# Issuing a weight sum behind the remainder of the unit ahead of it, in a four-layer trunk

## The chip, the cores and the metric

The kernel runs on one core of one Trainium2 chip. The metric is device microseconds (us) of that core, the median over the runs shown. TensorE is PE in the profile (PEld is its weight load), VectorE is DVE, ScalarE is ACT, GpSimd is POOL, and SyncE is SP.

## The reference

A residual stream of 256 tokens by 2048 channels passes a latent attention layer, an MLP, a state-space (Mamba-2) layer and a second MLP. All of it is float32. What the change touches are products of activations with large weights.

```python
def squared_relu_mlp(h, w_in, w_out):
    u = jax.nn.relu(h @ w_in)          # 2048 x 8192
    return (u * u) @ w_out             # 8192 x 2048

def ssm_mixer(h, w_in, ...):
    zxbcdt = h @ w_in                  # 2048 x 10304
    ...
    return y @ w_out

for i in range(DEPTH):                 # DEPTH = 2
    ...
    x = x + mix
    h = rms_norm(x, mlp_norm_g[i])
    x = x + squared_relu_mlp(h, mlp_w_in[i], mlp_w_out[i])
```

## The kernel before

**Weight units.** Weights stream in from HBM as units of 128x1024 float32 (512 KB, two blocks of 128x512). TensorE takes float32 operands in a reduced form (fp32r), so each unit is split: ScalarE writes an upper part `wh` (line 102), VectorE subtracts it from the raw weight and writes the remainder `wl` (line 103). A product then needs three matmuls, upper by upper, upper by remainder, and activation remainder by weight upper (lines 617 to 619 in the MLP, 1160 to 1162 in the state-space layer). A unit's matmuls follow a list that is fixed ahead of time. When TensorE's code takes unit j, the code for the split of unit j+3 is issued (`Flow.next`, with `ahead` giving how many units are loaded and split ahead). `wh` and `wl` have four buffers each, raw weights have six, so the split of a unit can only start when TensorE is done with the unit four places before it.

**Units with sums.** Eight column pairs of the first matrix of each MLP, seven of them woven with other work, and two pairs of the state-space input matrix are computed by a scheme of seven products in place of eight (`seven`). For one pair there are four slices d = 0 to 3, and for each slice four quarters of weights b11, b12, b21, b22. The units that the list takes in each slice, one after the other with other units between them, are

- M1: b11 as it was loaded, in a buffer of the pool `rx`;
- N7: b12 + b22, written over b22, both fresh from HBM, in two buffers of the pool `raw`;
- N5: b11 + b12, written over b12;
- N6: b11 + the new b22, written over b11. A GpSimd DMA (line 199) then accumulates b21 onto that buffer for the later unit N4;
- N4, M2 and N3 follow later, and need no VectorE sum.

Each sum is one VectorE instruction of 128x1024 (all have line 183, that of the helper `add`). The pairs of the MLPs are p = 1 to 7 in each of the two MLPs, those of the state-space layer are p = 0 and 1. That makes 56 + 8 = 64 rounds of M1, N7, N5, N6, so 64 sums for N7. In the profile a sum for N7 is the group `wraw<-wraw,wraw`, one for N5 `wraw<-wrx,wraw`, one for N6 `wrx<-wrx,wraw`.

**What sets the order.** TensorE's order is written out by hand (`manual_schedule`). On VectorE, ScalarE and the DMA queue of SyncE a scheduler of the framework places an instruction by its own estimate of when it can start. Once placed, each engine works through its queue in order, and an instruction that waits holds up all behind it. A call of `issue_after(ins)` adds an edge without a semaphore: what is issued inside it stands behind `ins` in the queue of that engine. `flow.last_lo` is the latest remainder (line 103) that was issued, which at the split of N7 is that of the unit before it in the list.

**Other work on the same queues.** Between the splits VectorE adds finished output blocks to the residual (`add_residual`, line 437), subtracts for the transposed hidden activations (line 300) and combines bank results (lines 621, 622). ScalarE has relu and square (577, 625, 567), the upper parts of the transposed activations (299), and a copy of the bank of M1 to SBUF at the end of a pair's M1 products (line 631, in `after`).

Of the kernel before, what the change touches and what calls it, by code (L numbers as in the profile page):

```python
# [71 lines left out]
class Flow:  # L72
# [22 lines left out]
    def halves(self, raw, n, step=None):  # L95

        nc = self.nc
        h = self.pools["wh"].tile([P, 1024], F32R, tag="wh", name=f"wh{self.done}")
        lo = self.pools["wl"].tile([P, 1024], F32R, tag="wl", name=f"wl{self.done}")
        for o in range(0, n, step or n):  # L100
            v = slice(o, o + (step or n))
            self.last = nc.scalar.activation(h[:, v], raw[:, v], AF.Copy)  # L102
            self.last_lo = nc.vector.tensor_tensor(lo[:, v], raw[:, v], h[:, v].bitcast(F32), ALU.subtract)  # L103
        return h, lo
# [65 lines left out]
def seven(prefix, p, src):  # L170

    state = {}

    def quarter(d, i, j):
        return src[2 * i + d // 2, 2 * p + j][:, (d % 2) * 1024:(d % 2) * 1024 + 1024]

    def unit(flow, name, d):  # L180
        nc = flow.nc
        st = state.setdefault(d, {})
        add = lambda out, a, b: nc.vector.tensor_tensor(st[out].tile, st[a].tile, st[b].tile, ALU.add)
        halves = lambda q: flow.halves(st[q].tile, 1024)

        def make():
            if name == "N7":
                add("b22", "b12", "b22")
                out = halves("b22")
                if d in LATE5:  # L190
                    nc.gpsimd.dma_start(st["b12"].tile, quarter(d, 0, 0), accum_op=ALU.add)
                return out
            if name == "N5" and d not in LATE5:
                add("b12", "b11", "b12")
                return halves("b12")
            if name == "N6":
                add("b11", "b11", "b22")
                out = halves("b11")
                nc.gpsimd.dma_start(st["b11"].tile, quarter(d, 1, 0), accum_op=ALU.add)  # L199
                return out  # L200
            return halves({"M1": "b11", "N4": "b11", "N5": "b12"}.get(name, name))

        def load(k, pool, q):
            st[k] = Load(pool, quarter(d, *q))
            return st[k]

        loads = {"M1": lambda: [load("b11", "rx", (0, 0))],
                 "N7": lambda: [load("b12", B12, (0, 1)), load("b22", "raw", (1, 1))],
                 "M2": lambda: [load("M2", "raw", (1, 0))], "N3": lambda: [load("N3", "raw", (1, 1))]}
        return Unit(prefix + (p, name, d), 2, 512, loads.get(name, list)(), make)  # L210

    return unit


class Trunk:
# [224 lines left out]
    def start(self, seq):  # L440
        nc, d = self.nc, self.d
        self.flow = Flow(nc, self.wp, seq, (6, 3))
        cst = self.c.tile([P, C_END], F32, name="cst")
        self.cst = cst
        self.ident_r = self.c.tile([P, P], F32R, name="ident")
        self.ident = self.ident_r.bitcast(F32)
        self.mhalf = self.c.tile([P, 16], F32, name="mhalf")
        warm = self.s2.tile([P, 512], F32R, tag="s2", name="warm")
        nc.vector.memset(warm.bitcast(F32), 1.0)
        bank = self.sm.tile([P, 512], F32, tag="sm", name="warmed")  # L450
        for _ in range(WARM):
            nc.tensor.matmul(bank, warm[:, :P], warm, start=True, stop=True)
        nc.gpsimd.memset(self.mhalf, -0.5)
        nc.scalar.dma_start(cst[:, C_G0:C_GQ], d["cst"][:, C_G0:C_GQ])
        nc.scalar.activation(self.stat(1), self.mhalf[:, :1], AF.Copy)
        raws = [self.ktile(self.k4, F32) for _ in range(4)]
        parts = [(0, slice(k, k + 1)) for k in range(4)] + [(1, slice(0, 2)), (1, slice(2, 4)), (2, slice(0, 4)), (3, slice(0, 4))]

        def some_x():
            j, k = parts.pop(0)  # L460
            nc.sync.dma_start(raws[j][:, k], d["xT"][j][:, k])

        self.flow.load(2, ((0, 512), (512, 1024)), some_x)
        for u in range(3, 7):
            some_x()
            self.flow.load(u)
        self.pos = self.c.tile([P, 2], I32, name="pos")
        self.x = [[self.res.tile([P, 512], F32, name=f"x{t}{n}") for n in range(4)] for t in range(2)]

        self.rs_pool = [self.c.tile([P, 4], F32, name=f"rs{i}") for i in range(2)]  # L470
        self.phase = 0
        self.xT = [(self.ktile(self.xtp), self.ktile(self.xtp)) for _ in range(4)]

        def split_x(j, ks):
            h, lo = self.xT[j]
            for k in ks:
                g = cst[:, C_G0 + 4 * j + k:C_G0 + 4 * j + k + 1]
                if (j, k) == (0, 0):
                    nc.vector.tensor_scalar(h[:, k], raws[j][:, k], g, None, ALU.mult)
                else:  # L480
                    nc.scalar.activation(h[:, k], raws[j][:, k], AF.Copy, scale=g)
                nc.vector.scalar_tensor_tensor(lo[:, k], raws[j][:, k], g, h[:, k].bitcast(F32), ALU.mult, ALU.subtract)

        split_x(0, (0,))
        self.flow.convert(1)
        split_x(0, (1, 2))
        self.flow.convert(2)
        split_x(0, (3,))
        self.flow.load(7)
        one = self.scratch()  # L490
        nc.sync.dma_start(one[:, :P], d["one"])
        nc.gpsimd.tensor_copy(self.ident_r, one[:, :P])
        nc.sync.dma_start(cst[:, C_GQ:], d["cst"][:, C_GQ:])
        nc.sync.dma_start(self.pos, d["pos"])
        split_x(1, range(4))
        ssq = self.stat(8)
        self.later(0, lambda: split_x(2, range(4)))
        self.later(1, lambda: split_x(3, range(4)))

        def stats(n):  # L500
            for t in range(2):
                nc.sync.dma_start(self.x[t][n], d["x"][t * P:(t + 1) * P, n * 512:(n + 1) * 512])
                self.square_sum(self.x[t][n], ssq[:, t * 4 + n:t * 4 + n + 1])
            if n == 3:
                self.set_rstd(ssq)

        for n, at in enumerate(X_AT):
            self.later(at, lambda n=n: stats(n))
# [1299 lines left out]
```

## Time and profile before

| | us |
|---|---|
| median of 3 runs | 2289.38 (2289.05 to 2290.42) |
| the profiled execution | 2292.69 |
| its span, first to last instruction | 2290.9 |
| mean granted TensorE clock | 0.999 |
| ACT busy | 1442.6 (63%) |
| POOL busy | 284.9 (12%) |
| HBM read | 542.23 MB |

A page of the profile gives busy time by engine, the chain of work that ended last, and groups of instructions by source line. In a group's row the numbers are count, busy us, mean ns of one, and the idle time of its engine just before it with what ended that. In the view of waits a row reads: engine, operation, what it waited for, us in total, times, longest. In the timeline a row reads: start, us, engine, line, operation, tiles, and in brackets the idle time before it. A "q" after an engine's name marks its instruction queue.

A matmul of 512 columns is shown with 0.39 us, but the next one starts 0.23 us later, since they overlap. So idle time of PE as shown is 0.16 us less than what was lost at that place.

### The profile page before, as it was taken

The page shows a single profiled execution, that of the slowest core. Times are in us where ns is not written, and L with a number is a line of the kernel's source. Part 1 is how long each engine was busy: PE and PEld are TensorE (multiplying, and loading weights), DVE is VectorE, ACT ScalarE, POOL GpSimd, SP SyncE. Part 2 cuts the span into 40 slices and gives each one's busy share as a digit, 9 for nine tenths or more (in the row PEclk, how much of TensorE's full clock was granted, in tenths as well). Part 3 has the DMA queues.
Part 4 walks back from the last instruction along what each step waited for, and adds up shares of the span by engine and source line. Part 5 has one row for each costly group of instructions (what it writes and reads, how often), then busy time and mean ns, then how long its engine had stood idle before and what let it go on. Part 6 is the DMA issues. An engine that isn't in the chain of part 4 may idle for free.

```text
span 2290.9 us, 30854 instructions
## 1 busy us (share of the span) xinstructions
PE 2273.1 (99%) x10881; PEld 1881.4 (82%) x10881; DVE 1964.4 (86%) x2257; ACT 1442.6 (63%) x2044; POOL 284.9 (12%) x339
## 2 busy tenths in 40 slices
PE   9999999999999999999999999999999999999999
PEld 7898888888888888887788788888888887888887
DVE  7786698999899897888889998976989988989985
ACT  7775476566566666566577676564666665666663
POOL 1440000000000000100002532230000000000000
PEclk9999999999999999999999999999999999999999
DMA  8545678888888877758798888866788887798874
GB/s 315 172 152 163 210 234 264 261 253 263 269 253 261 268 231 246 244 180 281 234 359 288 290 289 303 307 215 218 211 261 252 256 275 234 253 277 243 266 232 163
DMA packets 176026, 569.74 MB, mean 249 GB/s; under 512 B 20192, under 2 KB 29344, under 8 KB 175872
## 3 DMA queue, kind: packets, MB, share of 16 engines
q1 hardware_dynamic: 147808, 498.24, 64.9%
q0 software_dynamic: 16320, 56.88, 11.8%
q10 hardware_dynamic: 11744, 12.66, 1.7%
q8 instruction: 85, 1.39, 0.2%
q14 instruction: 69, 0.57, 0.1%
HBM read 542.23 MB, written 6.41 MB: 239 GB/s over the span
## 4 chain that ended last, share of the span: by engine, by line
PE 87%; DVE 6%; DMA 4%; issue 2%; ACT 1%; POOL 0%; SPq 0%; ACTq 0%; DVEq 0%
PE acc L339 10%; PE acc L340 10%; PE acc L343 10%; PE yp L618 9%; PE yp L619 8%; PE yp L617 8%; PE st L618 7%; PE st L619 7%; PE st L617 7%; DVE wl L103 3%; DMA wraw<-mi 2%; DMA wraw<-si 1%; ACT wh L102 1%; PE st L1162 1%; PE st L1160 1%
## 5 line engine op out<-in xcount | busy, mean ns | idle before, releaser
L102 ACT ACTIVATE wh<-wraw 128x1024 fp32r<-128x1024 f32 (+1 forms) x818 | 857.5, 1053 | 528.5 <-PE acc L340 176.7
L103 DVE TENSOR_TENSOR wl<-wraw,wh 128x1024 fp32r<-128x1024 f32 (+1 forms) x818 | 989.2, 1227 | 180.5 <-ACT wh L102 169.7
L617 PE MATMUL yp<-wh,k 128*128 128x512 f32 x896 | 349.7, 390 | 0.0
L618 PE MATMUL yp<-wl,k 128*128 128x512 f32 x896 | 349.1, 390 | 0.1
L619 PE MATMUL yp<-wh,k 128*128 128x512 f32 x896 | 349.0, 390 | 0.0
L102 ACT ACTIVATE wh<-wrx 128x1024 fp32r<-128x1024 f32 x192 | 203.2, 1059 | 174.8 <-PE yp L619 98.4
L103 DVE TENSOR_TENSOR wl<-wrx,wh 128x1024 fp32r<-128x1024 f32 x192 | 233.0, 1219 | 37.1 <-ACT wh L102 36.2
L618 PEld LDWEIGHTS yp<-wl,k 128*128 128x128 f32 x896 | 168.5, 188 | 35.5 <-DVE wl L103 0.5
L619 PEld LDWEIGHTS yp<-wh,k 128*128 128x128 f32 x896 | 168.5, 188 | 35.2
L339 PE MATMUL acc<-wh,k 128*128 128x512 f32 x496 | 196.9, 397 | 0.3 <-ACT k L299 0.3
L617 PEld LDWEIGHTS yp<-wh,k 128*128 128x128 f32 x896 | 168.5, 188 | 34.9
L340 PE MATMUL acc<-wh,k 128*128 128x512 f32 x496 | 193.7, 391 | 0.6 <-DVE k L300 0.6
L339 PE MATMUL acc<-wh,xt 128*128 128x512 f32 x480 | 191.8, 400 | 0.6 <-ACT wh L102 0.6
L340 PE MATMUL acc<-wh,xt 128*128 128x512 f32 x480 | 187.7, 391 | 0.0
L617 PE MATMUL st<-wh,xt 128*128 128x512 f32 x448 | 177.7, 397 | 0.0
L619 PE MATMUL st<-wh,xt 128*128 128x512 f32 x448 | 174.9, 390 | 0.0
L618 PE MATMUL st<-wl,xt 128*128 128x512 f32 x448 | 174.7, 390 | 0.0
L199 POOL DMA_DIRECT2D wrx<-mi x56 | 49.1, 877 | 726.1 <-DVE wl L103 515.5
L617 PE MATMUL st<-wh,sN 128*128 128x512 f32 x336 | 133.4, 397 | 0.8 <-ACT wh L102 0.8
L618 PE MATMUL st<-wl,sN 128*128 128x512 f32 x336 | 131.8, 392 | 2.1 <-DVE wl L103 2.0
L343 PE MATMUL acc<-wl,k 128*128 128x512 f32 x496 | 132.7, 389 | 0.0
L619 PE MATMUL st<-wh,sN 128*128 128x512 f32 x336 | 131.4, 391 | 0.0
(342 smaller groups left out, 3806.6 us busy)
## 6 DMA issues: line engine op xcount, KB each, us to landing
wraw<-mi SPq DMA_DIRECT2D x256, 512.0 KB, 5.7
wraw<-mo SPq DMA_DIRECT2D x256, 512.0 KB, 5.2
wraw<-si SPq DMA_DIRECT2D x160, 512.0 KB, 5.7
wraw<-so SPq DMA_DIRECT2D x64, 512.0 KB, 5.1
wrx<-mi SPq DMA_DIRECT2D x56, 512.0 KB, 5.2
wrx<-mi POOLq DMA_DIRECT2D x56, 512.0 KB, 7.7
wraw<-wo SPq DMA_DIRECT2D x32, 512.0 KB, 4.1
tap<-xD SPq DMA_DIRECT2D x24, 512.0 KB, 8.3
```

The source lines that it names most:

```text
L102: self.last = nc.scalar.activation(h[:, v], raw[:, v], AF.Copy)
L103: self.last_lo = nc.vector.tensor_tensor(lo[:, v], raw[:, v], h[:, v].bitcast(F32), ALU.subtract)
L199: nc.gpsimd.dma_start(st["b11"].tile, quarter(d, 1, 0), accum_op=ALU.add)
L339: nc.tensor.matmul(accs[t][:, :n], ah, wh[:, q, :], start=first and kt + q == 0, stop=False)
L340: nc.tensor.matmul(accs[t][:, :n], al, wh[:, q, :], start=False, stop=False)
L343: nc.tensor.matmul(accs[t][:, :n], lhs(kt + q, t)[0], wl[:, q, :], start=False, stop=en and q == nk - 1)
L617: nc.tensor.matmul(b, ah, wh, start=first and q == 0, stop=False)
L618: nc.tensor.matmul(b, ah, wl, start=False, stop=False)
L619: nc.tensor.matmul(b, al, wh, start=False, stop=last and q == 1)
L1160: nc.tensor.matmul(bank[onto], ah, wh, start=done + q == 0 and not skip, stop=False, skip_group_check=skip)
L1162: nc.tensor.matmul(bank[onto], ah, wl, start=False, stop=done == 3 and q == 1, skip_group_check=skip)
```

## The change

Two places change. The sum for N7 is issued inside `issue_after` with the last remainder, so it stands behind that remainder in VectorE's queue. The context is handed to the flow object.

```diff
         def make():
             if name == "N7":
-                add("b22", "b12", "b22")
+                with flow.tc.issue_after(flow.last_lo.ins):
+                    add("b22", "b12", "b22")
                 out = halves("b22")
...
         self.flow = Flow(nc, self.wp, seq, (6, 3))
+        self.flow.tc = self.tc
```

No instruction is added or removed. TensorE's and GpSimd's orders are the same, on SyncE one load moves (a b11 quarter of the state-space layer, behind four other loads). What moves on VectorE and ScalarE is shown at three places. Names carry buffer numbers that are the same in both kernels; line numbers above 188 are one or two higher in the changed kernel.

On VectorE, second half of pair 0 of the state-space layer (about 1049 to 1060 us in the trace of before). `wraw_9766` is the sum for N7 of slice d = 3, `wl_9729` the remainder of N5 and `wl_9742` that of N6 of slice d = 2, `wl_9789` that of M1 of slice 3. Before:

```order
L103 TENSOR_TENSOR wl_9711<-wraw_9669,wh_9710 128x1024
L183 TENSOR_TENSOR wrx_9655<-wrx_9655,wraw_9669 128x1024
L183 TENSOR_TENSOR wraw_9766<-wraw_9764,wraw_9766 128x1024
L103 TENSOR_TENSOR wl_9729<-wraw_9667,wh_9728 128x1024
L183 TENSOR_TENSOR wraw_9764<-wrx_9752,wraw_9764 128x1024
L103 TENSOR_TENSOR wl_9742<-wrx_9655,wh_9741 128x1024
L103 TENSOR_TENSOR wl_9755<-wraw_9707,wh_9754 128x1024
L103 TENSOR_TENSOR wl_9769<-wrx_9554,wh_9768 128x1024
L103 TENSOR_TENSOR wl_9779<-wraw_9738,wh_9778 128x1024
L103 TENSOR_TENSOR wl_9789<-wrx_9752,wh_9788 128x1024
```

The same place with the change:

```order
L103 TENSOR_TENSOR wl_9711<-wraw_9669,wh_9710 128x1024
L183 TENSOR_TENSOR wrx_9655<-wrx_9655,wraw_9669 128x1024
L103 TENSOR_TENSOR wl_9729<-wraw_9667,wh_9728 128x1024
L103 TENSOR_TENSOR wl_9742<-wrx_9655,wh_9741 128x1024
L103 TENSOR_TENSOR wl_9755<-wraw_9707,wh_9754 128x1024
L103 TENSOR_TENSOR wl_9769<-wrx_9554,wh_9768 128x1024
L103 TENSOR_TENSOR wl_9779<-wraw_9738,wh_9778 128x1024
L103 TENSOR_TENSOR wl_9789<-wrx_9752,wh_9788 128x1024
L183 TENSOR_TENSOR wraw_9766<-wraw_9764,wraw_9766 128x1024
L183 TENSOR_TENSOR wraw_9764<-wrx_9752,wraw_9764 128x1024
```

The sum for N7 moves behind six remainders, to its place behind M1's, and the sum for N5 moves with it.

On VectorE, pair 2 of the first MLP, slice d = 2 and what follows (about 504 to 513 us). `wl_5026`, `wl_5051` and `wl_5064` are the remainders of N7, N5 and N6, `wrx_4955` is the sum for N6, `x_142` and `x_146` are residual adds of a finished output block. Before:

```order
L183 TENSOR_TENSOR wrx_4955<-wrx_4955,wraw_4975 128x1024
L103 TENSOR_TENSOR wl_5026<-wraw_4975,wh_5025 128x1024
L103 TENSOR_TENSOR wl_5038<-wraw_4993,wh_5037 128x1024
L103 TENSOR_TENSOR wl_5051<-wraw_4973,wh_5050 128x1024
L103 TENSOR_TENSOR wl_5064<-wrx_4955,wh_5063 128x1024
L103 TENSOR_TENSOR wl_5075<-wraw_5035,wh_5074 128x1024
L437 TENSOR_TENSOR x_142<-yp_4953,x_142 128x512
L437 TENSOR_TENSOR x_146<-yp_4954,x_146 128x512
L183 TENSOR_TENSOR wraw_5106<-wraw_5104,wraw_5106 128x1024
```

With the change:

```order
L183 TENSOR_TENSOR wraw_4975<-wraw_4973,wraw_4975 128x1024
L183 TENSOR_TENSOR wraw_4973<-wrx_4955,wraw_4973 128x1024
L103 TENSOR_TENSOR wl_5026<-wraw_4975,wh_5025 128x1024
L103 TENSOR_TENSOR wl_5038<-wraw_4993,wh_5037 128x1024
L103 TENSOR_TENSOR wl_5051<-wraw_4973,wh_5050 128x1024
L183 TENSOR_TENSOR wrx_4955<-wrx_4955,wraw_4975 128x1024
L438 TENSOR_TENSOR x_142<-yp_4953,x_142 128x512
L438 TENSOR_TENSOR x_146<-yp_4954,x_146 128x512
L103 TENSOR_TENSOR wl_5064<-wrx_4955,wh_5063 128x1024
L103 TENSOR_TENSOR wl_5075<-wraw_5035,wh_5074 128x1024
```

All three sums stand later, and the two residual adds now stand ahead of the remainder of N6. This sequence (sum for N6, two residual adds, remainder of N6) stands in the changed order eight times, four times in each MLP, and never in the order of before.

On ScalarE, slice d = 3 of pair 1 of the first MLP (about 333 to 340 us). `wh_3578`, `wh_3598` and `wh_3611` are the upper parts of M1, N7 and N5, `s_451` is the copy of the bank of M1, which reads what TensorE finishes with M1's last matmul. Before:

```order
L102 ACTIVATE wh_3578<-wrx_3520 128x1024
L299 ACTIVATE k_445_3557<-sm_3588 128x4x128
L102 ACTIVATE wh_3598<-wraw_3535 128x1024
L102 ACTIVATE wh_3611<-wraw_3533 128x1024
L102 ACTIVATE wh_3623<-wrx_3343 128x1024
L631 ACTIVATE s_451_3633<-st_3319 128x512
L299 ACTIVATE k_445_3557<-sm_3635 128x4x128
```

With the change:

```order
L102 ACTIVATE wh_3578<-wrx_3520 128x1024
L300 ACTIVATE k_445_3557<-sm_3588 128x4x128
L633 ACTIVATE s_451_3633<-st_3319 128x512
L102 ACTIVATE wh_3598<-wraw_3535 128x1024
L300 ACTIVATE k_445_3557<-sm_3635 128x4x128
L102 ACTIVATE wh_3611<-wraw_3533 128x1024
L102 ACTIVATE wh_3623<-wrx_3343 128x1024
```

The copy of M1's bank moves ahead of three upper parts, and one upper part of activations ahead of two of them. Pair 1 of the second MLP has the same move.

## The prediction

> **What bounds the kernel.** I read the page first, then the waits of VectorE and of TensorE, then timelines at the places that they name.
>
> ```profile
> span 2290.9 us, 30854 instructions
> PE 2273.1 (99%) x10881; PEld 1881.4 (82%) x10881; DVE 1964.4 (86%) x2257; ACT 1442.6 (63%) x2044; POOL 284.9 (12%) x339
> ```
>
> TensorE is busy for all but 17.8 us of the span, so the kernel is bound by its matmuls, and a change of order can win only what TensorE loses in waits. VectorE comes second with 86%, and its queue is in order.
>
> ```profile
> DVE wraw L183 <- DMA wraw<-mi: 23.3, 25, 2.7
> DVE wraw L183 <- DMA wraw<-si: 11.7, 7, 3.1
> PE st L1162 <- DVE wl L103: 4.5, 5, 1.4
> PE st L618 <- DVE wl L103: 2.0, 4, 0.8
> PE st L617 <- ACT wh L102: 0.8, 1, 0.8
> PEld st L1162 <- DVE wl L103: 7.0, 6, 1.8
> PEld st L618 <- DVE wl L103: 4.9, 9, 1.1
> PEld st L617 <- ACT wh L102: 1.7, 2, 1.3
> ```
>
> Half of the 64 sums for N7 (25 + 7 rows) stand at the head of VectorE's queue before their weights have landed, and hold it for 35.0 us in total. TensorE feels little of that: 4.5 + 2.0 + 0.8 = 7.3 us of shown idle time at ten places where it wants a remainder or an upper part of a pair's unit. One of them in full, VectorE first:
>
> ```profile
> 1053.32 1.23 DVE L183 TENSOR_TENSOR wraw<-wraw,wraw 128x1024 f32<-128x1024 f32 x1 [2.30 <-DMA wraw<-si]
> 1054.46 1.22 DVE L103 TENSOR_TENSOR wl<-wraw,wh 128x1024 fp32r<-128x1024 f32 x1
> 1055.73 0.50 PE L1162 MATMUL st<-wl,sN 128*128 128x512 f32 x1 [1.40 <-DVE wl L103]
> ...
> 1061.27 1.22 DVE L103 TENSOR_TENSOR wl<-wrx,wh 128x1024 fp32r<-128x1024 f32 x1
> ```
>
> VectorE was free from 1051.02, stood 2.30 us in front of the sum, then summed, and only then made the remainder of N5 that TensorE was waiting for. The remainder ended at 1055.68 and the matmul began 0.05 us later; I use that handover below.
>
> **What the change removes.** At that place the order shows the sum behind six remainders, behind that of M1, which is the last row, some 8 us later; the longest wait of a sum was 3.1 us. So its data are there, and the remainder of N5 can start at 1051, over 3 us earlier than it did, which is more than the 1.56 us that TensorE lost (1.40 shown plus the 0.16 by which matmuls overlap). The other places are of the same kind. I count all ten as gone: 7.3 + 10 x 0.16 = 8.9 us. PEld's rows bound it from above: 17 weight loads waited 7.0 + 4.9 + 1.7 = 13.6 us, but a load that waits has usually a matmul still running beside it; the seven without an idle row of PE lost under 0.16 us each, 1.1 us in all. I take 10.0; the ends are 7.3 and 13.6.
>
> **What the half-rate stretch adds.** Right behind one of the ten stands a stretch at half clock.
>
> ```profile
> 1054.00:1058.00 4.00, 1.99 (x8) 1.05 (x6) 4.00 (x5) 1.86 (x2) 0.00 (x0) 1.00 0.47 125
> 1904.50:1908.50 4.00, 2.38 (x8) 1.43 (x9) 3.95 (x4) 2.80 (x4) 0.18 (x1) 1.00 0.71 218
> 1908.60:1911.90 3.30, 3.30 (x9) 2.51 (x8) 3.30 (x4) 2.54 (x3) 0.62 (x1) 0.50 0.72 119
> ```
>
> By column: stretch, its length, busy time of PE, PEld, DVE, ACT and POOL with counts, granted clock, DMA share, GB/s. After 4.0 us with PE busy for 2.38 it ran 3.30 us at clock 0.50, which loses half of it, 1.7 us. The same density at 1054 (1.99 of 4.0) had no such sequel, so it takes more than the density, and I cannot say what. The Trainium skill ("TensorE: Matmul & The Clock Gate", part 1 and its table of rules) has the clock fall after about an idle window of 3.4 us and warns of idle gaps above some 3 us. This trace fell to half after two shown gaps below 1 us each, so here the row decides; by the page no new half-rate stretch could follow from the gaps that I work out below, and the sum would be 0.85 us lower. I count the stretch as gone and as likely as not to come back once at one of the two new places: minus 0.85 us, ends minus 1.7 and plus 1.7.
>
> **What the change adds, first kind.** A sum that used to run early, while VectorE waited for ScalarE or the DMA, now runs after M1's remainder, and everything of that round after it. At eight places two residual adds now stand between the sum for N6 and its remainder.
>
> ```profile
> 508.36 1.22 DVE L103 TENSOR_TENSOR wl<-wrx,wh 128x1024 fp32r<-128x1024 f32 x1 [0.18 <-ACT wh L102]
> 510.81 1.28 DVE L437 TENSOR_TENSOR x<-yp,x 128x512 f32<-128x512 f32 x2
> 510.87 0.39 PE L619 MATMUL yp<-wh,k 128*128 128x512 f32 x1
> 512.68 0.39 PE L618 MATMUL st<-wl,sN 128*128 128x512 f32 x1
> ```
>
> Before, the remainder of N6 was done at 509.58, and TensorE read it at 512.68: over 3 us of margin. Now the second residual add has to wait for the last matmul of its bank, which ends at 510.87 + 0.39 = 511.26. VectorE takes the next instruction 0.60 us after that add's start (two take 1.28, so one takes 0.68 and they overlap by 0.08), at 511.87; the remainder needs 1.22, and with the handover TensorE can read it at 513.14: 0.46 us late. The order of TensorE is the same at all eight places, so 8 x 0.46 = 3.7 us. Below nothing it cannot go; if the scheduler's place for the adds costs their full 1.28 us each time, it is 10 us.
>
> **Second kind.** In slice 3 of pair 1 the copy of M1's bank has moved ahead of the upper parts of N7 and N5.
>
> ```profile
> 334.40 2.00 ACT L102 ACTIVATE wh<-wraw 128x1024 fp32r<-128x1024 f32 x2
> 337.65 0.60 ACT L631 ACTIVATE s<-st 128x512 f32<-128x512 f32 x1 [0.30 <-PE st L619]
> 338.15 0.59 ACT L299 ACTIVATE k<-sm 128x512 fp32r<-128x512 f32 x1
> 337.81 0.48 PE L617 MATMUL st<-wh,sN 128*128 128x512 f32 x1
> 338.13 0.40 PE L618 MATMUL st<-wl,sN 128*128 128x512 f32 x1
> 339.51 0.39 PE L618 MATMUL st<-wl,sN 128*128 128x512 f32 x1
> 1673.62 0.60 ACT L631 ACTIVATE s<-st 128x512 f32<-128x512 f32 x1 [0.32 <-PE st L619]
> 1673.78 0.48 PE L617 MATMUL st<-wh,sN 128*128 128x512 f32 x1
> ```
>
> The copy waits for TensorE's last matmul of M1 and cannot start before 337.65. Behind it ScalarE is free at 338.15. The upper part of N7, which used to run from 334.40, now runs from 338.15 for 1.05 (two take 2.00, one starts 0.95 after the other), to 339.20, and TensorE starts N7 at 339.24 in place of 337.81: 1.43 late. The remainder then runs 339.24 to 340.46 and is read at 340.51 in place of 338.13: 2.38 late. For N5, ScalarE first does the 0.59 of line 299 (from 339.10), then the upper part to about 340.6; VectorE has the matching subtraction of line 300 first, so the remainder of N5 starts near 341.0, ends at 342.2, and TensorE, which would want it at 339.51 + 2.38 = 341.89, loses 0.36 more. That is 2.74 us in the first MLP. In the second, copy and N7 stand the same 0.16 us apart, so 2.74 again. The sums just before add a few tenths in the first. I take 5.8 us for both; if the copy cost only its own place it would be 2 x 1.43 = 2.9, and at twice the working 11.
>
> **What hides the rest.** In the other MLP rounds the sum lies in VectorE time that is free, as the margin shows.
>
> ```profile
> 487.63 1.21 DVE L103 TENSOR_TENSOR wl<-wrx,wh 128x1024 fp32r<-128x1024 f32 x1
> 488.77 2.35 DVE L103 TENSOR_TENSOR wl<-wraw,wh 128x1024 fp32r<-128x1024 f32 x2
> 492.27 0.39 PE L618 MATMUL st<-wl,sN 128*128 128x512 f32 x1
> ```
>
> Here M1's remainder is followed by N7's, done at 488.77 + 1.21 = 489.98 and read at 492.27, 2.29 us later. With the change the sum (1.14 from start to start), the upper part (1.05) and the remainder (1.22) follow M1's remainder in series, 3.4 us and two handovers behind its end at 488.84: 492.35. That would be 0.1 us late if M1's remainder stayed where it is. But the sums for N7 and N5, which stood ahead of it, have moved behind it, so M1's remainder can come up to 2 x 1.14 = 2.3 us earlier, and I expect a margin above 1 us. I cost the 46 rounds of this kind at nothing, and so the eight rounds of the state-space pairs, where six remainders stand ahead of the sum and the margin is wider. The cover is that margin; if it is gone, the second rival below has the price.
>
> ```profile
> wraw<-mi SPq DMA_DIRECT2D x256, 512.0 KB, 5.7
> ```
>
> Raw buffers are now read later by their sums, and so come free later, and one load is issued behind four others. A load lands 5.7 us after its issue (median), and the sums waited for theirs only because they stood so early; I cost both at nothing.
>
> **The sum.** Minus 10.0 minus 0.85 plus 3.7 plus 5.8 is minus 1.4 us on the profiled execution's own 2292.69, so 2291.3. Carried to the median of the runs, 2289.38, which is 3.3 lower, it gives 2288.0.
>
> **Rivals.** First: only the gain appears, because VectorE and ScalarE, no longer held for 35.0 us, reach the ten added places early enough. For it speaks the size of the 35.0; against it, both added waits hang on TensorE's own last matmul, which no earlier VectorE changes. Price: minus 10.0 and minus 1.7, so 2277.7. Chance 0.15, a part of it with some of the added waits left.
>
> Second, on the other side: the series sum, upper part, remainder uses up the margin in all rounds. It decides once M1's remainder does not come earlier by at least the 0.1 us above. With 0.3 us lost in each of the 46 rounds it adds 13.8 us: 2301.8. For it speaks that VectorE shows 86% over the whole span; against it, the removed 35.0 us. Chance 0.09.
>
> Third: the change does not do what it says, the queue still stands for the DMA at the new place, and only the added 9.5 us show: 2298.9. Against it, a sum waited at most 3.1 us and moved by more than that. Chance 0.04.
>
> **Chances.** My forecast has 0.72, with its own range 2284 to 2292. A measurement of this kernel can tell about 0.2%, or 4.6 us, from no change. Faster than 2284.8 takes the first rival and 0.05 of the forecast: 0.20. Slower than 2294.0 takes the other two rivals less their mildest part: 0.12. The rest is 0.68. The range runs from 2280.5, which takes in the milder half of the first rival, to 2293.5.
>
> **What would show it.** The rows of the sum for N7 waiting for a DMA should be gone from VectorE's waits, and PE's idle rows at lines 1162 and 618 near 1055, 1102, 1117, 1908 and 1994 with them. New idle rows should stand at eight reads of N6 remainders (near 513), 0.3 us each as shown, and at N7 in slice 3 of pair 1 near 339 and 1675, over 1 us each for upper part and remainder. I am wrong if the ten old waits stay, if rounds other than those ten show PE waiting for line 103, or if more half-rate stretches appear than one.

## The result, and the profile after

The changed kernel takes 2292.86 us (median of 22 runs, 2289.72 to 2297.09) beside 2289.22 us for the kernel before (22 runs, 2287.05 to 2294.09). The ratio is 1.0014 with a 95% interval of 1.0007 to 1.002, so the change costs 3.2 us (1.6 to 4.6). (The ratio is taken over all the runs of both, so it is not quite that of the two medians, which lie 3.6 us apart; all differences below go by such ratios.) The forecast was a gain of 1.4 us; the time lies inside the range, on the other side of no change.

The profiles of the two kernels say something else at first sight. The span of the changed kernel's is 2290.2 us, 0.7 us shorter than that of the one before.

```profile
span 2290.2 us, 30868 instructions
PE 2273.2 (99%) x10881; PEld 1881.4 (82%) x10881; DVE 1968.2 (86%) x2257; ACT 1434.2 (63%) x2044; POOL 284.5 (12%) x339
```

In the view of waits, the rows of a sum for N7 waiting for a DMA are gone from VectorE's, and TensorE's rows of the state-space pairs with them. What is left of TensorE's waits in the pairs is this:

```profile
PE st L620 <- DVE wl L103: 4.6, 12, 0.8
PE st L619 <- ACT wh L102: 2.4, 2, 1.2
```

That is 7.0 us shown, fourteen waits at ten places, where before it was 7.3 us in ten waits: old waits went, new ones came. In the state-space pair that the prediction shows, VectorE (timeline, start and length in us) now makes four remainders in a row and finds the sum's data there:

```profile
1048.80 2.35 DVE L103 TENSOR_TENSOR wl<-wraw,wh 128x1024 fp32r<-128x1024 f32 x2
1051.07 2.35 DVE L103 TENSOR_TENSOR wl<-wrx,wh 128x1024 fp32r<-128x1024 f32 x2
1053.34 1.22 DVE L183 TENSOR_TENSOR wraw<-wraw,wraw 128x1024 f32<-128x1024 f32 x1
```

The first of the two sorts of new waits, pair 2 of the first MLP (TensorE is some 4.6 us later here than in the trace of before):

```profile
515.22 1.37 DVE L438 TENSOR_TENSOR x<-yp,x 128x512 f32<-128x512 f32 x2 [0.25 <-PE yp L621]
516.50 1.22 DVE L103 TENSOR_TENSOR wl<-wrx,wh 128x1024 fp32r<-128x1024 f32 x1
517.06 0.39 PE L619 MATMUL st<-wh,sN 128*128 128x512 f32 x1
517.78 0.50 PE L620 MATMUL st<-wl,sN 128*128 128x512 f32 x1 [0.33 <-DVE wl L103]
518.11 0.39 PE L621 MATMUL st<-wh,sN 128*128 128x512 f32 x1
```

The residual adds wait for TensorE's last matmul of their bank, the remainder of N6 comes behind them, and TensorE loses 0.33 + 0.16 = 0.49 us at the read of it. Eight places show it. But that is not the whole loss. The same three matmuls in the profile of before:

```profile
512.45 0.39 PE L617 MATMUL st<-wh,sN 128*128 128x512 f32 x1
512.68 0.39 PE L618 MATMUL st<-wl,sN 128*128 128x512 f32 x1
512.91 0.39 PE L619 MATMUL st<-wh,sN 128*128 128x512 f32 x1
```

From the first to the third it took 0.46 us before and takes 1.05 now: the matmul behind the one that waited starts 0.33 us after it in place of 0.23, so each such place costs 0.6 us. (The section on the profile before puts the loss at 0.16 us above the idle time shown; at these waits it is some 0.26.)

The second sort, slice 3 of pair 1, ScalarE and TensorE:

```profile
338.26 0.60 ACT L633 ACTIVATE s<-st 128x512 f32<-128x512 f32 x1 [2.72 <-PE st L621]
338.76 1.05 ACT L102 ACTIVATE wh<-wraw 128x1024 fp32r<-128x1024 f32 x1
339.86 0.49 PE L619 MATMUL st<-wh,sN 128*128 128x512 f32 x1 [1.19 <-ACT wh L102]
341.12 0.80 PE L620 MATMUL st<-wl,sN 128*128 128x512 f32 x1 [0.77 <-DVE wl L103]
341.71 0.63 PE L621 MATMUL st<-wh,sN 128*128 128x512 f32 x1
342.14 0.63 PE L619 MATMUL st<-wh,sN 128*128 128x512 f32 x1
```

ScalarE waits 2.72 us for the copy with the upper part of N7 behind it. But the copy is only the last of two things in the way. The upper part of N7 reads the sum for N7, and VectorE makes that sum now only behind M1's remainder, with the sum for N5 next:

```profile
337.03 1.22 DVE L183 TENSOR_TENSOR wraw<-wraw,wraw 128x1024 f32<-128x1024 f32 x1
338.27 1.23 DVE L183 TENSOR_TENSOR wraw<-wrx,wraw 128x1024 f32<-128x1024 f32 x1
339.84 1.23 DVE L103 TENSOR_TENSOR wl<-wraw,wh 128x1024 fp32r<-128x1024 f32 x1 [0.34 <-ACT wh L102]
```

The sum ends at 338.25, so with no copy ahead of it the upper part could have started some 0.5 us earlier than at 338.76, and no more. From 341.12 the matmuls are 0.63 us long in place of 0.39, which is half clock. The view by stretches (columns as in the prediction) has it, here in the first profile and in a second one of the same kernel (label a2_after):

```profile
341.00:344.20 3.20, 3.08 (x7) 2.51 (x8) 3.20 (x5) 2.67 (x4) 0.00 (x0) 0.50 0.16 20
```

```profile
341.60:344.80 3.20, 3.20 (x9) 2.43 (x9) 3.20 (x3) 2.51 (x3) 0.00 (x0) 0.50 0.26 68
1672.00:1676.00 4.00, 2.32 (x12) 1.48 (x10) 3.63 (x4) 2.57 (x4) 0.00 (x0) 1.00 0.80 153
1676.20:1679.40 3.20, 3.12 (x7) 2.48 (x8) 3.20 (x5) 2.67 (x4) 0.00 (x0) 0.50 0.15 24
```

So the waits of the profile stand at the places foreseen. The question is why the runs lose 3.2 us where the profiles show 0.7 us of gain.

### The profile page after: what moved, and what is told of

It reads as the page before. It is cut to its first block, busy times and chain, and to the rows that moved or that the text cites. A ratio compares the mean times of both kernels' runs of the same rounds, so it can differ in the third digit from the quotient of the medians.

```text
span 2290.2 us, 30868 instructions
## 1 busy us (share of the span) xinstructions
PE 2273.2 (99%) x10881; PEld 1881.4 (82%) x10881; DVE 1968.2 (86%) x2257; ACT 1434.2 (63%) x2044; POOL 284.5 (12%) x339
## 3 DMA queue, kind: packets, MB, share of 16 engines
q0 software_dynamic: 16320, 56.88, 11.5%
## 4 chain that ended last, share of the span: by engine, by line
PE 96%; DVE 2%; ACT 1%; DMA 1%; issue 1%; POOL 0%; ACTq 0%; SPq 0%; DVEq 0%
PE acc L340 10%; PE acc L341 10%; PE acc L344 10%; PE yp L619 9%; PE yp L620 9%; PE yp L621 9%; PE st L620 8%; PE st L621 7%; PE st L619 7%; PE st L1164 1%; PE st L1163 1%; PE st L1162 1%; PE yp L340 1%; PE yp L341 1%; PE yp L344 1%; DVE wl L103 1%
```

## The experiments

Every experiment limits the new order to some rounds, by a condition at the one place of the change:

```diff
-                with flow.tc.issue_after(flow.last_lo.ins):
+                with flow.tc.issue_after(flow.last_lo.ins) if COND else nullcontext():
                     add("b22", "b12", "b22")
```

The results are ratios to the kernel before on the same chip. A wait of TensorE's is counted from the start of one matmul to the start of the next, less the usual 0.23 us. A loss "between the same matmuls" is the time from one matmul to a later one in one profile, against the same two in another; that can be done because TensorE's order is the same in all of these kernels, and it takes in the late matmul behind a wait as well. "SSM" stands for the state-space pairs.

**e1_ssm**: COND is `len(prefix) == 1`.

> The sum stands behind the remainder in the eight rounds of the state-space pairs only. Theory A (the waits that the profile of before shows are in the timed runs as well): the waits at 1055 to 1117 go, 5.3 us, so 0.2 to 0.25% faster than before (ratio 0.9975 to 0.998). Theory B (the late loads in front of the sums belong to the profiled execution and hardly occur in the timed runs): no difference, ratio 0.9995 to 1.0005. In the profile itself both expect the waits gone and the span 5 us shorter.

Measured: 2282.93 against 2290.73 us, ratio 0.9967 (0.9954 to 0.9979), 7.6 us faster. That is more than A's 0.9975, which the interval still holds. The waits that the profile shows in the state-space pairs are in the runs too, and theory B falls.

**e2_mlp**: COND is `len(prefix) == 2`.

> The sum stands behind the remainder in the 56 rounds of the MLPs only. Theory A: 9.5 us of added waits, 4.5 us of removed ones, one half-rate stretch of 1.7 us removed and one or two added: plus 5 to 7 us, ratio 1.002 to 1.003. Theory B: nothing is removed, so 9.5 us and one or two half-rate stretches: plus 11 to 13 us, ratio 1.005 to 1.0057.

Measured: 2300.25 us, ratio 1.0036 (1.0023 to 1.0048), 8.2 us slower. B lies outside; A's 1.002 to 1.003 overlaps the interval, below its middle. All of the loss, and more, is in the MLPs.

**e3_pair1**: COND is `len(prefix) == 2 and p == 1`.

> Only in pair 1 of each MLP (eight rounds). Both theories: the two places with the copy of M1's bank, 5.6 us, and with each a half-rate stretch (1.7 us) in some of the executions: plus 5.6 to 9 us, ratio 1.0025 to 1.004. This prices the second kind of added wait.

Measured: 2298.04 us, ratio 1.0032 (1.002 to 1.0044), 7.3 us slower. Eight of 64 rounds carry most of the loss of the MLPs. In the profile the two places cost 3.4 and 4.7 us between the same matmuls, the second with a half-rate stretch behind it.

**e4_rest**: COND is `len(prefix) == 2 and p > 1`.

> Only in pairs 2 to 7 of each MLP (48 rounds). Theory A: eight waits of 0.47 us added (3.8 us), 4.5 us removed and a half-rate stretch of 1.7 us removed: minus 2.4 us, ratio 0.999. Theory B: plus 3.8 us, ratio 1.0017.

Measured: 2292.77 us, ratio 1.0008 (0.9999 to 1.0017). It lies between the theories: the eight added waits are there (0.49 us each at the read, 0.6 with the matmul behind it), and something is removed, but by the time not the 6.3 us that A takes from the profile of before.

```profile
PE st L1164 <- DVE wl L103: 4.3, 6, 1.1
PE st L620 <- DVE wl L103: 2.7, 8, 0.3
```

Line 1164 is the state-space pairs, as before; line 620 is the MLPs, eight places and nothing else.

By then the profiles of e1 and e3, in which the old order stands in pairs 2 to 7, showed old waits of 3.3 and 2.4 us there, not 4.6, and no half-rate stretch behind them. So for the next batch theory F stands for "the first profile of before is typical", and G for "what it shows in the MLPs changes from execution to execution".

**e6_slice1**: COND is `len(prefix) == 2 and p > 1 and d == 1`. In this order neither the copy nor the residual adds have moved ahead.

> Only slice 1 of pairs 2 to 7 of the MLPs: the gain of the MLPs by itself. Theory F (the profile of before is typical: waits of 4.6 us near 737, 1904 to 1908, 1994, 2078, and a half-rate stretch of 1.7 us): minus 6.3 us, ratio 0.9973. Theory G (these waits and the stretch change from execution to execution, the profiles of the first batch show 2.4 to 3.3 us and no stretch there): minus 2.5 to 4, ratio 0.9983 to 0.999.

Measured: 2286.7 against 2290.89 us, ratio 0.9982 (0.9973 to 0.9991), 4.1 us faster. The value lies 0.1 us outside G's range, and F's stands at the edge of the interval. The view of waits has no row of line 620 left: slice 1 alone removes every old wait of the MLPs, and adds none. What remains of TensorE's waits in its pairs:

```profile
PE st L1164 <- DVE wl L103: 4.6, 6, 1.8
```

**e7_slice3**: COND is `len(prefix) == 2 and p == 1 and d == 3`.

> Only slice 3 of pair 1 of the two MLPs, two sums in all. The copy of M1's bank stands behind N7's upper part and ahead of N5's. Worked by the same rows as in the prediction: 2.5 us of waits at each of two places, 5 us. Theory F (a half-rate stretch is as likely as not): plus 5.9. Theory G (one of the two places has a stretch in each execution, since its windows run free of the program): plus 6.7 us, ratio 1.0029, and a stretch at clock 0.50 behind one of the places in the profile.

Measured: 2295.06 us, ratio 1.0021 (1.0012 to 1.003), 4.8 us slower. Between the same matmuls each of the two places costs 2.5 us in the profile, the 5 us worked out. Here the copy stands behind the upper part of N7, and yet 2.5 of the 3.3 us that the full change costs at such a place without a half-rate stretch are left. VectorE, then ScalarE:

```profile
335.56 1.21 DVE L183 TENSOR_TENSOR wraw<-wraw,wraw 128x1024 f32<-128x1024 f32 x1
336.81 1.23 DVE L183 TENSOR_TENSOR wraw<-wrx,wraw 128x1024 f32<-128x1024 f32 x1
337.95 1.22 DVE L103 TENSOR_TENSOR wl<-wraw,wh 128x1024 fp32r<-128x1024 f32 x1
336.81 1.06 ACT L102 ACTIVATE wh<-wraw 128x1024 fp32r<-128x1024 f32 x1 [2.54 <-DVE wraw L183]
```

ScalarE waits 2.54 us for the sum itself, and the remainder of N7 follows the two sums on VectorE without a pause. So most of the second sort of wait comes from where the sums stand; how much of the rest is the copy's is not shown. There was no half-rate stretch in the profile, so G's "one in each execution" missed. The reason may be how the gaps lie:

```profile
339.22 0.50 PE L620 MATMUL st<-wl,sN 128*128 128x512 f32 x1 [0.81 <-DVE wl L103]
341.50 0.50 PE L620 MATMUL st<-wl,sN 128*128 128x512 f32 x1 [0.61 <-DVE wl L103]
```

Here the larger gaps stand 2.3 us apart, with the full change 1.3 us apart and one of them longer.

**a2_after**: the changed kernel once more.

> The changed kernel once more, beside the others on one chip, and a second profile of it. Theory F: ratio 0.9994. Theory G: between 1.0005 and 1.002, the two sorts of added waits at the same ten places within 0.05 us, and one half-rate stretch or more.

Measured: 2292.69 against 2290.89 us, ratio 1.0007 (0.9998 to 1.0016); F's 0.9994 is outside. TensorE's waits in the pairs are the two rows of the first profile, 4.6 us at twelve reads and 2.4 us at two, and two half-rate stretches are shown above.

**l1_before, l2_before, l3_before, l4_after**: one execution of each, for the spread between executions.

> The kernel before, unchanged, for a second profile. If the first profile is typical: waits at the places near 737, 1904 to 1908, 1994 and 2078 of 4.4 to 4.8 us in all and a half-rate stretch near 1909. If they change from execution to execution, as theory G has it: 2.4 to 3.7 us there and no such stretch; the waits of the state-space pairs between 4.3 and 5.7 us in either case.

> A third profile of the changed kernel. Theory G: ten added waits of 9.9 to 10.1 us in all, the same as in its other two profiles to 0.1 us, none of the old ones, and one or two half-rate stretches behind slice 3 of pair 1.

l2_before and l3_before had the expectations of l1_before. Rows of TensorE's waits in the MLPs' pairs, from l1, l2 and l3:

```profile
PE st L618 <- DVE wl L103: 0.6, 1, 0.6
```

```profile
PE st L618 <- DVE wl L103: 1.8, 4, 0.8
```

```profile
PE st L618 <- DVE wl L103: 2.1, 4, 0.7
```

The table has all the profiles in which the old order stands at the place. The columns of waits count from start to start, above 0.14 us each. Those of the losses are between the same matmuls, beside profiles in which no old wait is left at the place (e5 and e6 for the MLPs, the changed kernel for the state-space pairs), without the half-rate stretch.

| profile | span | waits, MLPs | half-rate stretch behind them | waits, SSM | loss, MLPs | loss, SSM |
|---|---|---|---|---|---|---|
| before, that of the prediction | 2290.9 | 4.4 | 1 | 6.3 | 5.2 | 6.5 |
| l1_before | 2287.8 | 1.0 | 0 | 5.6 | 1.8 | 5.6 |
| l2_before | 2291.1 | 3.0 | 0 | 6.7 | 3.9 | 6.7 |
| l3_before | 2286.1 | 2.7 | 0 | 5.1 | 3.4 | 5.2 |
| e1_ssm | 2281.2 | 3.3 | 0 | removed | 3.8 | removed |
| e3_pair1 | 2295.3 | 2.4 | 0 | 5.3 | 3.2 | 5.5 |
| e7_slice3 | 2292.4 | 3.7 | 0 | 6.6 | 4.5 | 6.8 |
| e2, e4, e6 | | removed | | 6.2, 6.3, 6.5 | removed | 6.3, 6.4, 6.7 |

The profile that the prediction was made from has the largest loss of the seven in the MLPs, and the only stretch (1.6 us more). l1 fell below G's 2.4 us. Each sum of waits of the state-space pairs holds one of 1.0 us at line 339 (340 in changed kernels), of which 0.7 us stays with the change; without it l1 to l3 have 4.6, 5.7 and 4.1 us, where 4.3 to 5.7 was expected. l4_after has the same two rows of waits as the first profile of the changed kernel, and one stretch, as G said. In the five profiles where the full change stands in pair 1 (the changed kernel three times, e2, e3) there are six stretches behind its slice 3, at one place or at both.

The timed executions tell of stretches too, since each has its mean granted clock on record, to three places. One stretch of 3.4 us at half clock takes 1.7 us of some 2290 and brings the mean to 0.9993; 0.998 takes two or more.

| granted clock | 1.000 | 0.999 | 0.998 | mean time lost, us (from the rounded clocks) |
|---|---|---|---|---|
| changed kernel, 33 executions | 7 | 13 | 13 | 2.7 |
| before, beside the experiments, 43 executions | 19 | 24 | 0 | 1.3 |

So the changed kernel loses 1.4 us more to the clock in the mean of its executions (standard error 0.35 us; on one chip, 11 beside 27, it is 2.7 beside 1.4). For e3 it is 2.1 us more than for the kernel before on its chip (six executions, standard error 1.0), for e7 nothing.

**e5_pick**, which beats both kernels: COND is `len(prefix) == 1 or p > 1 and d == 1`, the state-space pairs and slice 1.

> The sum stands behind the remainder in the state-space pairs and, of the MLPs, only in slice 1 of pairs 2 to 7, where sums waited for loads ahead of a wait of TensorE; the order then has neither the copy ahead of upper parts nor two residual adds ahead of the remainder of N6. Both theories: the state-space gain of the first batch (7.6 us) and whatever slice 1 gives: 9.5 to 14 us faster than before, ratio 0.994 to 0.996, the fastest of all kernels here.

Measured: 2279.16 against 2290.89 us, ratio 0.995 (0.9938 to 0.9963), 11.5 us faster. It was expected between 9.5 and 14, and is close to the sum of e1 (7.6) and e6 (4.1). Thirteen sums for N7 still wait for their loads, 11.9 us in all, and none of it reaches TensorE, whose waits have no row of a pair left:

```profile
DVE wraw L183 <- DMA wraw<-mi: 11.9, 13, 1.5
```

## Why the prediction was wrong

**What bounds the kernel, and what sits where**, was right. The waits of the sums are gone, the waits behind them too, and new ones stand at the ten places foreseen and nowhere else in the pairs.

**First kind of added wait**: 0.46 us was worked out for the read that waits, 0.49 measured. With the matmul behind it a place costs 0.6 us, and the eight cost 5.2 us between the same matmuls (5.1 to 5.3 in five profiles) for 3.7. The prediction left that matmul out, here and in the waits removed.

**Second kind**: 2.74 us and some tenths were worked out for each place, 3.3 measured where no stretch lies on it, so 6.7 us for 5.8. The upper part of N7 came 1.44 us late for 1.43, its remainder 0.94 more for 0.95, that of N5 0.24 more for 0.36. The rest is 0.36 at a remainder ahead of them, in both MLPs, and 0.1 behind each of three waits. The steps were right in size, but the cause was right only in part. The copy is what ScalarE waits for last, yet e7 keeps 2.5 of the 3.3 us with the copy behind the upper part: the two sums that the change puts in front of the remainder of N7 hold it up by themselves. That a working by the copy alone came so close is in part luck, since the sum ends only some 0.5 us before the copy.

**The cover of the other rounds** held. At the place shown in the prediction, the remainder of N7 now ends 1.06 us before TensorE reads it:

```profile
494.59 2.36 DVE L103 TENSOR_TENSOR wl<-wraw,wh 128x1024 fp32r<-128x1024 f32 x2
496.87 0.39 PE L620 MATMUL st<-wl,sN 128*128 128x512 f32 x1
```

(494.59 + 1.22 = 495.81.) So the second rival, a loss in all rounds, had the right sign and the wrong mechanism.

**What failed is the step on the half-rate stretch.** It counted the old one as gone (minus 1.7 us) and as likely as not to come back once (plus 0.85). The old one is in one of seven profiles, so on average the change removes 0.2 us. The new ones are six in five profiles; each adds 1.1 to 1.3 us between the same matmuls, less than the 1.7 since part of it lies on a wait, so 1.5 us in each execution. In place of minus 0.85 the step is plus 1.3, an error of 2.1 us. More than one stretch was also the prediction's own sign of being wrong, and a2_after has two. The recorded clocks of the timed executions say the same: 1.4 us more lost with the change. The Trainium skill ("TensorE: Matmul & The Clock Gate", part 1) has the clock judged over a window of some 3.4 us that runs free of the program; the stretches here are 3.4 us long or twice that in the records of the granted clock, and come or not in the same wait of the same kernel, which fits. Its rule about idle gaps above 3 us does not: no gap in pair 1 is shown longer than 1.2 us.

**The second error is in sizes.** The added waits were worked out 2.4 us too small, by the matmul behind each wait and by the tenths ahead of the second kind. The removed waits were taken as 10.0 us. Over the table they average 3.7 us in the MLPs and 6.2 in the state-space pairs, 9.9 us, so this term came out, but by luck: the profile that it was read from lost 11.8 us to them. The count was short by 1.8 us, and that execution had 1.9 us more than the mean.

This answers the question of the result. In the first profile of before the old waits and the stretch cost 13.4 us, in that of the changed kernel the new waits and the stretch 12.9; but the 13.4 is 3.3 us above the mean of the profiles. The removed losses differ from one execution to the next, by 3.4 us in the MLPs and 1.6 in the state-space pairs; the added waits of the first kind agree within 0.2 us, and those of the second within 0.1 where no stretch lies on them.

| term | forecast | mean over the profiles, between the same matmuls |
|---|---|---|
| old waits removed | -10.0 | -9.9 |
| half-rate stretches, old and new | -0.85 | +1.3 |
| first kind | +3.7 | +5.2 |
| second kind | +5.8 | +6.7 |
| sum, before rounding | -1.4 | +3.2 |

The same terms, taken for the places that each kernel changes, can be set against its timed runs:

| kernel | from the terms, us | timed, us |
|---|---|---|
| changed kernel | +3.2 | +3.2 (1.6 to 4.6); a2: +1.6 (-0.5 to 3.7) |
| e1_ssm | -6.2 | -7.6 (-10.5 to -4.8) |
| e2_mlp | +9.4 | +8.2 (5.3 to 11.0) |
| e3_pair1 | +8.2 | +7.3 (4.6 to 10.1) |
| e4_rest | +1.3 | +1.8 (-0.2 to 3.9) |
| e5_pick | -10.1 | -11.5 (-14.2 to -8.5) |
| e6_slice1 | -3.9 | -4.1 (-6.2 to -2.1) |
| e7_slice3 | +5.0 | +4.8 (2.7 to 6.9) |

All lie inside their intervals. The terms rest on five to nine profiles, among them those of the kernels in the table, so this is a test of the sums more than of each term. By themselves the timed runs show the gain of the state-space pairs (e1), the gain of slice 1 (e6), the loss of pair 1 (e3), most of it from one sum in each MLP (e7), and by their clocks the share of the stretches.

## What to carry to other kernels

Moving an instruction that waits for a load behind one that does not is worth what its wait costs the bound engine, place by place. Put it only there: the same edge at places without a cost held up a remainder that TensorE read next, and let a scheduler put other work ahead of it. When waits hang on loads, one profile is a sample of them; take several before their sum is set against waits that the order fixes. Where the order of the bound engine is the same in both kernels, count what a wait costs from one matmul to a later one, in both profiles.

## What the runs showed of the hardware that was not expected

Half-rate stretches of the TensorE clock followed two gaps of 0.8 to 1.2 us shown, 1.6 to 2.0 us together, within about 2.5 us, and not each time. A longer wait, near 1268 us at line 343 (344 in the changed kernels; 1.5 to 3.3 us), was followed by a stretch in some profiles and by none in others; in l2_before and in e2_mlp it lasted twice as long, 6.8 us in the records of the clock (l2_before):

```profile
1264.50:1268.30 3.80, 0.92 (x5) 0.42 (x3) 3.80 (x7) 2.17 (x3) 1.16 (x3) 0.95 0.61 202
1268.50:1274.50 6.00, 5.91 (x69) 4.96 (x70) 6.00 (x7) 3.86 (x8) 0.29 (x1) 0.50 0.63 188
```

It stood in five of the nine profiles with the old order in the state-space pairs, and in one of the five with the new. Between the same matmuls this place took 1.4 us less with the new order in the state-space pairs, in the mean of these profiles, but with the old order it differs by 4.7 us from one execution to another. Whether the change has a part in that stays open; if it has all of it, the sum of the terms above is 1.8 us in place of 3.2, and that for e1 minus 7.6.
